# One accumulator on VectorE for the weighted sum of gathered expert rows, in place of two on three engines

## The chip, the cores and the metric

The kernel runs on one core of one Trainium2 chip. The metric is the device time of one execution in microseconds, the median of several runs.

## The reference

A backbone of two layers over 512 latent tokens with 256 context tokens, d = 1024. Each layer mixes tokens and then runs a product-key expert network (PEER) on each token: a router picks 16 of 16384 experts for each of 8 heads, 128 rows a token, and the token's output is a gated, weighted sum over them. That last step is what the change touches:

```python
u_e = u_tab[ib]                                   # ib: [tokens, 8, 16] of 16384 experts
v_e = v_tab[ib]
a = jax.nn.gelu(jnp.einsum('nd,nhkd->nhk', xb, u_e)) * gb
return jnp.einsum('nhk,nhkd->nd', a, v_e)
```

Layer 0 does it for latent and context tokens, layer 1 for latent tokens alone.

## The kernel before

**Two ways through the experts.** Most latent tokens take all 16384 experts, with a gate that is zero for the experts not picked: in layer 0 all 512 tokens (four tiles of 128), in layer 1 the first 384 (three tiles). The other tiles gather the rows that the router picked: the two context tiles in layer 0, the last latent tile in layer 1.

**The dense way** has two stages. `build_g` writes the gates of all experts to DRAM, with comparisons on VectorE (L1364, L1365), products on VectorE (L1366) and GpSimd or VectorE (L1370, `go`), and TensorE products in float16. `dense` then goes over 128 blocks of 128 experts. For each it loads `du` and `dv` (512 KB each), makes the two float32r parts of each (`duh` on ScalarE L1388, `dul` on VectorE L1389, `dvh` L1461, `dvl` L1462), and forms the activations `h` by 24 matmuls (`hidden`, L1394). Every fifth block's activations were made earlier, beside the routing, and are kept in DRAM; these 26 blocks load them as `dge` instead, so 102 blocks have the 24 matmuls. VectorE multiplies with the gates (`dcf`, L1469), ScalarE and VectorE make the two parts `dch` (L1472) and `dcl` (L1473), and TensorE multiplies with `v` into `o` (L142): 18 matmuls for three tiles of tokens into six PSUM banks, which stay there to the end. In layer 0 the fourth tile has no banks for that: `fourth()` (L1427) takes it for a pair of blocks at a time, in one bank, and VectorE adds the bank to `do` in SBUF (L1436) before the next use of the bank. That makes 24 matmuls of `o` a block in layer 0.

**The gathered way** runs in the background of both stages. `gather` (L1209) is a generator; a step of it issues the two indirect fetches of group n on GpSimd (L1258; a row of 8 KB for each of 128 tokens, u and v side by side in one `uv` tile), the products of group n-1 with the token (VectorE, L1240: an elementwise product over the u half with its sum into `dots`), gelu and gate (ScalarE L1244, VectorE L1252), and the weighted sum of group n-2. There are 128 rows a tile in groups of two, so 64 steps. Of each group, the even row is scaled by ScalarE in place (L1226) and added by GpSimd to `acc[1]` (L1227; the first row of the tile is written there by ScalarE alone, L1229); the odd row is scaled and added by VectorE in one instruction to `acc[0]` (L1232, first row L1234). After the last step VectorE joins the two (L1263), multiplies with the gate row (L1265) and adds the residual (L1267). The six `uv` buffers hold three groups.

**What sets the order.** Steps are called while the program of the stage is written: in `build_g` by a rate a piece of the gates (L1369), in `dense` after each block's `dch` and `dcl` so that all are done six blocks before the end (L1474 to L1477). A scheduler then sets the order of each engine's queue, and each engine runs its queue in order. `du` and `dv` and the other plain loads are issued by SyncE, the fetches by GpSimd.

Of the kernel before, what the change touches and what calls it, by code (L numbers as in the profile page):

```python
# [15 lines left out]
AF = mybir.ActivationFunctionType  # L16
OP = mybir.AluOpType
# [4 lines left out]
P = 128  # L22
D = 1024
# [18 lines left out]
# latent tokens whose experts are computed densely, per layer; the rest gathers expert rows  # L42
# [22 lines left out]
# candidate pairs (a, b) of two sorted lists with (a + 1)(b + 1) <= 16: (first a, number of a, number of b, offset)  # L65
# [10 lines left out]
def merge(*gens):  # L76
    """Steps of several generators in turn."""
    gens = list(gens)
    while gens:
        for g in list(gens):  # L80
            try:
                yield next(g)
            except StopIteration:
                gens.remove(g)


class Kern:
    def __init__(self, ctx, tc, a, dbg=None):
# [12 lines left out]
        self.split = lambda k: k % 2 == 0  # L101
# [43 lines left out]
    def tick(self, us):  # L145
        """Advance the background work by what fits beside `us` of foreground work."""
# [23 lines left out]
    def steps(self, n):  # L170
        """Advance the background work by n steps."""
        self.pace += n
        while self.pace >= 1.0:
            self.pace -= 1.0
            self.step()

    def flush(self):
        """Finish the gathers under way without starting others."""
# [5 lines left out]
    def advance(self, n):  # L184
        """Advance the second background work by n steps."""
# [29 lines left out]
    # ------------------------------------------------------------------ setup  # L215
# [34 lines left out]
    def xsrc(self, l, w, seg, i, cols=slice(0, D)):  # L250
        """Residual stream before sub-layer w of layer l: 128 tokens of a segment."""
# [15 lines left out]
    # -------------------------------------------------------------------- ada  # L267
    def ada(self, l, parts, pw, ps):
        """Modulation vectors: shifts and scales as columns, gates as rows in DRAM."""
# [10 lines left out]
        for part in parts:  # L280
            for half in range(2):
# [4 lines left out]
                # a quarter of the array for each of four blocks of the contraction  # L286
# [28 lines left out]
    # ------------------------------------------------------------ adaLN norms  # L315
    def parts(self, pool, src, cols, tag, eng, bufs):
        """Half a block of weights in the two parts that float32r products carry: a pair for each 128 rows."""
# [7 lines left out]
    def norm(self, l, w, seg, xT, xt=None, side=None, deep=2):  # L325
        """Modulated norm, channel-major, of the residual stream, in one part or two.

        xt: the stream [P, n / P, D] and partial sums of its squares [P, n / P, 4], where those are on chip."""
# [40 lines left out]
    # ------------------------------------------------------------- token mix  # L369
# [3 lines left out]
    def store(self, l, seg, full, st, m, alias=False):  # L373
        """What outlives the projections, in a pool for each of three stacks."""
# [25 lines left out]
    def projections(self, l, seg, full, m):  # L400
        """The projections of a segment, a generator that takes a block of weights in each step."""
# [17 lines left out]
    def latent(self, l, m):  # L419
        """The first layer's latent projections, then their attention where the projections' operand was."""  # L420
# [6 lines left out]
    def mlstm(self, l, seg, full, m):  # L427
        """The recurrence after the projections, a generator."""
# [12 lines left out]
    def project_ctx(self, l, m):  # L441
        """The context's new residual stream, to DRAM."""
# [20 lines left out]
    def project(self, l, m, px, sd, rest=()):  # L463
        """The latent tokens' new residual stream, to DRAM and to a pool, after the rest of their mixing."""
# [41 lines left out]
    def weights(self, l, full, pool):  # L506
        """Blocks of columns of w_in (256, the gates 100), each a step; half a block ahead of its use."""
# [20 lines left out]
    def mm3(self, out, lhs, rhs):  # L528
        """Contraction over blocks of operands that are given in two parts each."""
# [6 lines left out]
    def chan(self, w, c, m, x):  # L536
        """Channel-major projections of m columns from column c of the weight block."""
# [5 lines left out]
    def rows(self, w, i, x):  # L543
        """Token-major projections of a tile of tokens."""
# [5 lines left out]
    def tseq(self, ap, seg):  # L550
        """A channel-major row of a segment in its token order, viewed in time order."""
# [5 lines left out]
    # ----------------------------------------------------------------- mLSTM  # L557
    def ml_proj(self, l, seg, full, x, m):
        """Queries, keys, values and output gates, a generator."""
# [69 lines left out]
    def ml_gin(self, l, seg, x, m):  # L629
        """Gate preactivations in time order (reversed for the backward direction)."""  # L630
# [86 lines left out]
    def ml_core(self, l, seg, full, m):  # L717
        """Chunked recurrence of both directions, a generator."""
# [3 lines left out]
    def ml_chunks(self, st, l, seg, full, m):  # L722
# [14 lines left out]
        # recurrent states before each chunk, in the order of processing  # L737
# [124 lines left out]
    # --------------------------------------------------------------- pooling  # L862
# [42 lines left out]
    # ------------------------------------------------ neighbourhood attention  # L905
    def na_proj(self, l, seg, full, x, d):
        """Normalised queries (token-major) and keys (channel-major) and values, a generator."""
# [4 lines left out]
        with ExitStack() as st:  # L912
# [25 lines left out]
            # the keys' transposes come where the tensor engine need not wait for them  # L938
# [14 lines left out]
    def na_core(self, l, seg, d, sd):  # L953
        """Attention of all heads, a generator; each step's softmax runs beside the products of its neighbours."""
# [95 lines left out]
    # ------------------------------------------------------------------ PEER  # L1050
    def route(self, l, seg, xT, pr):
        """Product-key top-k of each token: expert ids [P, HK] and gates [P, HK] per tile."""
# [80 lines left out]
    def route_pick(self, pw, nt, sf, iv, iota, h0, ts, ef):  # L1133
        """Best TOPK pairs of RH heads from their sorted lists: scores and expert ids, in three steps."""
# [74 lines left out]
    def gather(self, pg, l, seg, i, xn, idx, gate):  # L1209
        """Experts of one tile of tokens by gathered rows, a generator over groups of experts."""  # L1210
# [458 lines left out]
```

## Time and profile before

| | |
|---|---|
| runs | 4574.12, 4580.28, 4576.12 us, median 4576.12 us |
| the profiled execution: its span | 4588.3 us (no other time of it is recorded) |
| TensorE matmul (PE) | 4041.2 us busy, 88% of the span |
| VectorE (DVE) | 3483.2 us, 76% |
| GpSimd (POOL) | 2233.7 us, 49% |
| ScalarE (ACT) | 1761.3 us, 38% |
| gathered fetches, their DMA queue | 406.35 MB, 24.2% of the 16 engines' span |

The profiled execution is 0.27% longer than the median of the runs. Busy times are sums over one execution; engines run beside each other. A matmul's record is longer than the distance to the next one, since matmuls overlap. PEclk is the clock that TensorE was granted, as a share of 2.4 GHz. The stages of interest are, in layer 0, the building of the gates up to 1302 us and the dense stage from 1302 to 2690; in layer 1 the same up to 3580 and from there to the end. A line of `L142` is that of a helper that issues most matmuls; the tile names tell them apart.

### The profile page before, as it was taken

The numbers are of one execution on the slowest core, as the hardware profiler recorded it, in microseconds if no ns is written. First come the engines' busy times: TensorE is split into PE (matmuls) and PEld (weight loads), VectorE is DVE, ScalarE is ACT, GpSimd is POOL, SyncE is SP. The second block draws the span as 40 slices with busy tenths as digits, with TensorE's granted clock in tenths as the row PEclk, the third lists the DMA queues.
The fourth block names the chain that finished last, engine by engine and source line by source line (L and its number), as shares of the span: only waits on it lengthen the run. The fifth ranks groups of instructions, "written<-read, shape, count | busy, mean of one in ns | idle before, by whom it ended". The sixth has DMA issues, their size and how long they took to land. (4 is left out here: it accounts for less than half of the span.)

```text
span 4588.3 us, 57862 instructions
## 1 busy us (share of the span) xinstructions
PE 4041.2 (88%) x20829; PEld 3367.6 (73%) x20829; DVE 3483.2 (76%) x6158; ACT 1761.3 (38%) x2754; POOL 2233.7 (49%) x1552
## 2 busy tenths in 40 slices
PE   6889777877779999999999979888868899999998
PEld 4568667756657777777777768677657788888887
DVE  2545675789979999889999855674889678887776
ACT  2332243335543333333333333343246344444343
POOL 2133355776645555455555333345866344444441
PEclk8889888988889999999999989988978999999999
DMA  7663212327778888788888633223256777777784
GB/s 270 215 211 93 81 48 82 94 94 227 219 268 303 323 316 317 301 316 316 322 316 317 257 113 109 63 73 98 71 171 206 263 294 291 286 301 296 277 304 166
DMA packets 429352, 996.51 MB, mean 217 GB/s; under 512 B 31448, under 2 KB 264280, under 8 KB 375816
## 3 DMA queue, kind: packets, MB, share of 16 engines
q1 hardware_dynamic: 372760, 586.46, 37.0%
q0 software_dynamic: 56304, 406.35, 24.2%
q8 instruction: 164, 2.69, 0.2%
q14 instruction: 124, 1.02, 0.1%
HBM read 909.97 MB, written 81.17 MB: 216 GB/s over the span
## 5 line engine op out<-in xcount | busy, mean ns | idle before, releaser
L1227 POOL TENSOR_TENSOR eacc<-eacc,uv 128x1024 f32<-128x1024 f32 x189 | 587.2, 3107 | 1074.1 <-ACT uv L1226 1013.4
L1240 DVE SCALAR_TENSOR_TENSOR uv<-uv,xn 128x1024 f32<-128x1024 f32 x384 | 849.8, 2247 | 0.0
L142 PE MATMUL o<-dvh,dch 128*128 128x512 f32 x1792 | 709.0, 396 | 72.3 <-DVE do L1436 53.2
L142 PE MATMUL o<-dvh,dcl 128*128 128x512 f32 x1792 | 706.0, 394 | 0.7 <-DVE dcl L1473 0.7
L142 PE MATMUL o<-dvl,dch 128*128 128x512 f32 x1792 | 704.9, 393 | 0.0
L1258 POOL DMA_INDIRECT uv<-in_peer_uv_dram,ridx x384 | 579.7, 1510 | 137.2 <-issue 75.0
L1394 PE MATMUL h<-xh,duh 128*128 128x512 f32 (+1 forms) x1632 | 607.7, 372 | 37.2 <-ACT duh L1388 35.8
L1394 PE MATMUL h<-xh,dul 128*128 128x512 f32 (+1 forms) x1632 | 607.6, 372 | 0.4 <-DVE dul L1389 0.3
L1394 PE MATMUL h<-xl,duh 128*128 128x512 f32 (+1 forms) x1632 | 606.0, 371 | 0.0
L142 PEld LDWEIGHTS o<-dvh,dch 128*128 128x128 f32 x1792 | 337.2, 188 | 162.1 <-DVE do L1436 64.6
L142 PEld LDWEIGHTS o<-dvh,dcl 128*128 128x128 f32 x1792 | 338.2, 189 | 86.9 <-DVE dcl L1473 14.6
L142 PEld LDWEIGHTS o<-dvl,dch 128*128 128x128 f32 x1792 | 337.5, 188 | 66.7 <-DVE dvl L1462 0.3
L1394 PEld LDWEIGHTS h<-xh,duh 128*128 128x128 f32 x1632 | 312.6, 192 | 80.4 <-ACT duh L1388 36.4
L1462 DVE TENSOR_TENSOR dvl<-dv,dvh 128x1024 fp32r<-128x1024 f32 x256 | 309.8, 1216 | 62.5 <-ACT dvh L1461 62.4
L1389 DVE TENSOR_TENSOR dul<-du,duh 128x1024 fp32r<-128x1024 f32 x204 | 249.5, 1224 | 135.0 <-ACT duh L1388 128.2
L1388 ACT CAST duh<-du 128x1024 fp32r<-128x1024 f32 x256 | 267.6, 1046 | 202.7 <-PE h L1394 102.1
L1394 PEld LDWEIGHTS h<-xl,duh 128*128 128x128 f32 x1632 | 312.1, 191 | 43.6
L1394 PEld LDWEIGHTS h<-xh,dul 128*128 128x128 f32 x1632 | 311.2, 191 | 39.7 <-DVE dul L1389 1.6
L142 PE MATMUL mm<-go,gob 128*128 128x128 f16 x1792 | 239.9, 297 | 96.9 <-DVE go L1366 85.4
L1244 ACT ACTIVATE egf<-dots 128x2 f32<-128x2 f32 x192 | 39.1, 204 | 734.8 <-DVE uv L1240 734.8
L1472 ACT CAST dch<-dcf 128x512 fp32r<-128x512 f32 (+1 forms) x256 | 145.2, 567 | 437.1 <-DVE dcf L1469 434.8
L1461 ACT CAST dvh<-dv 128x1024 fp32r<-128x1024 f32 x256 | 263.2, 1048 | 112.1 <-DMA dv<-in_peer_v_dram 63.4
(356 smaller groups left out, 8785.2 us busy)
## 6 DMA issues: line engine op xcount, KB each, us to landing
du<-in_peer_ut_dram SPq DMA_DIRECT2D x256, 512.0 KB
dv<-in_peer_v_dram SPq DMA_DIRECT2D x256, 512.0 KB
Gd<-gst SPq DMA_DIRECT2D x28, 2048.0 KB
wa<-in_w_ada_dram SPq DMA_DIRECT2D x24, 2048.0 KB
w<-in_w_in_dram SPq DMA_DIRECT2D x78, 512.0 KB
dG<-Gd SPq DMA_DIRECT2D x32, 1024.0 KB
w<-in_peer_wq_dram SPq DMA_DIRECT2D x48, 512.0 KB
dG<-Gd SPq DMA_DIRECT2D x32, 768.0 KB
```

Of the source, the lines that this page charges most:

```text
L142: self.nc.tensor.matmul(out, lhsT=lhsT, rhs=rhs, start=start, stop=stop)
L1227: nc.gpsimd.tensor_add(acc[1], acc[1], V)
L1240: nc.vector.scalar_tensor_tensor(t[:, :D], t[:, :D], 1.0, xn, op0=OP.mult, op1=OP.mult, accum_out=dots[:, k:k + 1])
L1244: nc.scalar.activation(ge, x, AF.Gelu_apprx_tanh)
L1258: nc.gpsimd.indirect_dma_start(t, None, a["peer_uv"], bass.IndirectOffsetOnAxis(ap=idx[:, k:k + 1], axis=0))
L1388: nc.scalar.copy(uh, u)
L1389: eng.tensor_sub(ul, u, uh.bitcast(F32))
L1394: nc.tensor.matmul(hp[:, :nd], lhsT=lt[:, k], rhs=rt[:, k, :nd], start=n == 0, stop=n == 3 * KD - 1)
L1461: nc.scalar.copy(vh, v)
L1462: nc.vector.tensor_sub(vl, v, vh.bitcast(F32))
L1472: m1 = nc.scalar.copy(ch, cf)
```

## The change

All rows of a gathered tile go to one accumulator. Each row is scaled and added by one VectorE instruction; ScalarE's scaling, GpSimd's addition, the second accumulator, the choice between them (`self.split`) and the joining addition are gone:

```diff
-        self.split = lambda k: k % 2 == 0
...
-        acc = [T(pg, [P, D], tag="eacc0"), T(pg, [P, D], tag="eacc1")]
-        used = [False, False]
+        acc = T(pg, [P, D], tag="eacc")
+        used = False
...
             for k, t, w in done:
-                V = t[:, D:]
-                if self.split(k):
-                    if used[1]:
-                        nc.scalar.activation(V, V, AF.Copy, scale=w)
-                        nc.gpsimd.tensor_add(acc[1], acc[1], V)
-                    else:
-                        nc.scalar.activation(acc[1], V, AF.Copy, scale=w)
-                    used[1] = True
-                elif used[0]:
-                    nc.vector.scalar_tensor_tensor(acc[0], V, w, acc[0], op0=OP.mult, op1=OP.add)
+                if used:
+                    nc.vector.scalar_tensor_tensor(acc, t[:, D:], w, acc, op0=OP.mult, op1=OP.add)
                 else:
-                    nc.vector.tensor_scalar_mul(acc[0], V, w)
-                    used[0] = True
+                    nc.vector.tensor_scalar_mul(acc, t[:, D:], w)
+                used = True
...
-        if used[1]:
-            nc.vector.tensor_add(acc[0], acc[0], acc[1])
         self.load(xn, self.grow[l][1][seg:seg + 1, :].to_broadcast([P, D]))
-        nc.vector.tensor_mul(acc[0], acc[0], xn)
+        nc.vector.tensor_mul(acc, acc, xn)
         self.load(xn, self.xsrc(l, 1, seg, i))
-        nc.vector.tensor_add(acc[0], acc[0], xn)
-        self.load(self.xdst(l, 1, seg, i), acc[0])
+        nc.vector.tensor_add(acc, acc, xn)
+        self.load(self.xdst(l, 1, seg, i), acc)
```

The rest of the diff empties comments. Lines behind the change stand some 11 lower: the product with the token is L1231 (before L1240), the multiply-add L1223 (L1232), the gate L1243 (L1252), the fetch L1249 (L1258), `do` L1425 (L1436), `dvl` L1451 (L1462), `dcl` L1462 (L1473).

Two places of the engines' queues show what moves. The first is VectorE in the dense stage of layer 0, one step of the gather; `eacc` is the accumulator, `uv` a gathered row, `egf` its weight. Before:

```order
L1473 TENSOR_TENSOR dcl_13903<-dcf_13900,dch_13902 128x512
L1232 SCALAR_TENSOR_TENSOR eacc_1861_8864<-uv_13750,egf_13836,eacc_1861_8864 128x1024
L1240 SCALAR_TENSOR_TENSOR uv_13839,dots_8863<-uv_13839,xn_4947 128x1024
L1240 SCALAR_TENSOR_TENSOR uv_13841,dots_8863<-uv_13841,xn_4947 128x1024
L1436 TENSOR_TENSOR do_2355_11271<-do_2355_11271,o_13944 128x512
L1462 TENSOR_TENSOR dvl_13955<-dv_13952,dvh_13954 128x1024
L1252 TENSOR_TENSOR egf_13911<-egf_13911,rgate_1077_4928 128x2
L1462 TENSOR_TENSOR dvl_14032<-dv_14029,dvh_14031 128x1024
```

With the change:

```order
L1462 TENSOR_TENSOR dcl_13861<-dcf_13858,dch_13860 128x512
L1223 SCALAR_TENSOR_TENSOR eacc_8864<-uv_13707,egf_13794,eacc_8864 128x1024
L1231 SCALAR_TENSOR_TENSOR uv_13797,dots_8863<-uv_13797,xn_4947 128x1024
L1223 SCALAR_TENSOR_TENSOR eacc_8864<-uv_13709,egf_13794,eacc_8864 128x1024
L1231 SCALAR_TENSOR_TENSOR uv_13799,dots_8863<-uv_13799,xn_4947 128x1024
L1425 TENSOR_TENSOR do_2354_11263<-do_2354_11263,o_13901 128x512
L1243 TENSOR_TENSOR egf_13868<-egf_13868,rgate_1077_4928 128x2
L1451 TENSOR_TENSOR dvl_13912<-dv_13909,dvh_13911 128x1024
L1451 TENSOR_TENSOR dvl_13988<-dv_13985,dvh_13987 128x1024
```

Each of the two products with the token now stands behind a multiply-add into the same accumulator, and the second multiply-add has one product between itself and the first.

The second is GpSimd in the dense stage of layer 0; in brackets are the semaphores of the engines and DMA queues that an instruction waits for. Before:

```order
L1227 TENSOR_TENSOR eacc_3169_15584<-eacc_3169_15584,uv_16759 128x1024 [waits DMASW0_49,Activation_49]
L1258 DMA uv_17002<-in_peer_uv_dram,ridx_1079_4936 128x2048 [waits DMASW1_49,DVE_49]
L1258 DMA uv_17004<-in_peer_uv_dram,ridx_1079_4936 128x2048 [waits Pool_49]
L1227 TENSOR_TENSOR eacc_3169_15584<-eacc_3169_15584,uv_16836 128x1024 [waits DMASW2_49,Activation_49]
L1258 DMA uv_17093<-in_peer_uv_dram,ridx_1079_4936 128x2048 [waits DMASW3_49,DVE_49]
```

With the change:

```order
L1249 DMA uv_16081<-in_peer_uv_dram,ridx_1079_4936 128x2048 [waits DMASW2_49,DVE_49]
L1249 DMA uv_16083<-in_peer_uv_dram,ridx_1079_4936 128x2048 [waits DMASW3_49,DVE_49]
L1249 DMA uv_16157<-in_peer_uv_dram,ridx_1079_4936 128x2048 [waits DMASW4_49,DVE_49]
L1249 DMA uv_16159<-in_peer_uv_dram,ridx_1079_4936 128x2048 [waits DMASW5_49,DVE_49]
L1249 DMA uv_16247<-in_peer_uv_dram,ridx_1079_4936 128x2048 [waits DMASW6_49,DVE_49]
```

Before, each pair of fetches stood behind an addition that waits for ScalarE; now fetches stand behind fetches, and each of them waits for VectorE itself.

## Rows read from the trace of the kernel before

**Rows 1.** Stretches: us; PE, PEld, DVE, ACT, POOL busy; PEclk, DMA, GB/s
```profile
1010.00:1302.00 292.00, 229.66 (x1395) 183.14 (x1395) 281.31 (x296) 164.78 (x192) 184.31 (x86) 0.87 0.72 221
1302.00:2690.00 1388.00, 1307.99 (x5520) 1052.05 (x5520) 1212.68 (x1347) 511.96 (x700) 702.63 (x365) 0.97 0.79 300
...
3580.00:4588.00 1008.00, 975.25 (x4752) 862.05 (x4752) 768.40 (x868) 408.79 (x583) 406.69 (x183) 0.99 0.75 277
```

**Rows 2.** Waits of PE, 1302 to 2690: us, times, longest
```profile
PE o L142 <- DVE do L1436: 53.2, 27, 3.1
PE h L1394 <- ACT duh L1388: 21.3, 1, 21.3
```

**Rows 3.** Groups of DVE, 1302 to 2690: busy us, mean ns, idle
```profile
L1240 DVE SCALAR_TENSOR_TENSOR uv<-uv,xn 128x1024 f32<-128x1024 f32 x238 | 537.5, 2293 | 0.0
...
L1232 DVE SCALAR_TENSOR_TENSOR eacc<-uv,egf,eacc 128x1024 f32<-128x1024 f32 x119 | 152.1, 1278 | 0.0
```

**Rows 4.** Timeline of DVE, one step: start us, us, line, tiles
```profile
1705.47 1.28 DVE L1232 SCALAR_TENSOR_TENSOR eacc<-uv,egf,eacc 128x1024 f32<-128x1024 f32 x1
1706.67 3.44 DVE L1240 SCALAR_TENSOR_TENSOR uv<-uv,xn 128x1024 f32<-128x1024 f32 x1
...
1710.04 1.21 DVE L1240 SCALAR_TENSOR_TENSOR uv<-uv,xn 128x1024 f32<-128x1024 f32 x1
1711.18 0.08 DVE L1240 DVE_READ_ACCUMULATOR uv<-uv,xn 128x1 f32 x1
```

**Rows 5.** Timeline of POOL beside it
```profile
1705.96 3.06 POOL L1227 TENSOR_TENSOR eacc<-eacc,uv 128x1024 f32<-128x1024 f32 x1 [5.82 <-ACT uv L1226]
```

**Rows 6.** Timeline of PE, two waits (idle before in brackets)
```profile
1713.22 0.50 PE L142 MATMUL o<-dvh,dch 128*128 128x512 f32 x1 [2.25 <-DVE do L1436]
...
1777.04 0.61 PE L142 MATMUL o<-dvh,dch 128*128 128x512 f32 x1 [2.61 <-DVE do L1436]
```

**Rows 7.** Timeline of DVE, the end of a gathered tile
```profile
1925.76 1.22 DVE L1263 TENSOR_TENSOR eacc<-eacc,eacc 128x1024 f32<-128x1024 f32 x1
1927.01 1.23 DVE L1265 TENSOR_TENSOR eacc<-eacc,xn 128x1024 f32<-128x1024 f32 x1
```

**Rows 8.** Timeline of PE, the ends of one block's `h` products
```profile
1683.19 0.40 PE L1394 MATMUL h<-xh,duh 128*128 128x512 f32 x1
...
1688.80 0.40 PE L142 MATMUL o<-dvh,dch 128*128 128x512 f32 x1
```

**Rows 9.** Chain of waits: 36 products of `o`; start us, us
```profile
3625.38 8.20 PE o L142 x36
```

**Rows 10.** Stretches in layer 0, columns as in rows 1
```profile
1777.30:1780.70 3.40, 3.40 (x9) 2.61 (x9) 3.40 (x3) 2.67 (x3) 2.53 (x1) 0.50 0.94 343
1780.70:1883.10 102.40, 98.22 (x425) 79.33 (x425) 94.29 (x107) 38.03 (x55) 56.87 (x30) 1.00 0.84 321
2000.00:2020.00 20.00, 18.25 (x80) 14.54 (x79) 16.87 (x17) 7.04 (x9) 9.19 (x6) 1.00 1.01 404
```

**Rows 11.** Groups of POOL, 3580 to 4588
```profile
L1227 POOL TENSOR_TENSOR eacc<-eacc,uv 128x1024 f32<-128x1024 f32 x62 | 186.6, 3009 | 533.2 <-ACT uv L1226 520.0 <-issue 13.2
```

**Rows 12.** Waits of PE, 3580 to 4588
```profile
PE o L142 <- ACT dch L1472: 15.7, 24, 1.2
```

**Rows 13.** Chain of waits, 3998 to 4080
```profile
4008.20 4.49 DVE uv L1240 x4
...
4014.24 8.39 DMA dge<-H
...
4034.09 4.52 PE o L142 x18
```

**Rows 14.** Groups of POOL, 1010 to 1302
```profile
L1227 POOL TENSOR_TENSOR eacc<-eacc,uv 128x1024 f32<-128x1024 f32 x7 | 19.9, 2838 | 1.3 <-DVE go L1366 1.3
```

**Rows 15.** Timeline of DVE in layer 1
```profile
4012.61 1.21 DVE L1462 TENSOR_TENSOR dvl<-dv,dvh 128x1024 fp32r<-128x1024 f32 x1
```

**Rows 16.** Timeline of POOL in layer 1
```profile
4012.67 1.97 POOL L1258 DMA_INDIRECT uv<-in_peer_uv_dram,ridx  x1 [0.30 <-issue]
```

## The prediction

> **What bounds the kernel now.** I read the stretches first [rows 1]: the gathers run in two pairs of stages, the building of the dense gates and then the dense experts, once a layer. In the dense stage of layer 0 (1302 to 2690 us) VectorE is busy 1212.7 of 1388 us and the clock share is 0.97; in that of layer 1 (from 3580) it is busy 768.4 of 1008 and the clock is 0.99. TensorE is the longest engine in both, so the next view is what it waits for. In layer 0 that is 53.2 us in 27 waits for `do`, VectorE's addition of the fourth token tile, beside one wait of 21.3 us at the start [rows 2]. So VectorE, in its order, sets the end there.
>
> What VectorE does in that time is in the groups by form [rows 3]: 238 products with the token (L1240) at a mean of 2293 ns, against 119 multiply-adds into the accumulator (L1232) of the same size at 1278 ns. The timeline of one step shows why [rows 4]: of two equal products the first takes 3.44 us, the second 1.21. GpSimd's addition starts at 1705.96 and takes 3.06, to 1709.02 [rows 5]; the first product starts inside it and ends at 1710.11, 1.1 us after it, which is about its own length. VectorE stands while GpSimd adds. The step of VectorE from L1232 to the end of the second product is 1.20 + 3.37 + 1.14 = 5.71 us from start to start (1705.47, 1706.67, 1710.04, 1711.18 in [rows 4]). TensorE waits for the queue behind it: it has stood 2.25 us for `do` at 1713.22, and 64 us later it has stood 2.61 us once more [rows 6].
>
> **The change part by part.** *Removed:* three tiles of 64 steps each lose a scaling on ScalarE and an addition on GpSimd a step (189 additions, since a tile's first row only starts the sum), and a joining addition each. ScalarE is not what is waited for, so its part is worth nothing by itself. GpSimd's part is worth the stall: 3.37 - 1.14 = 2.23 us in each step. *Added: one multiply-add on VectorE in each step*, 1.20 us from start to start [rows 4]. The new order of a step is accumulator, product, accumulator, product: 1.20 + 1.14 + 1.20 + 1.14 = 4.68 us, or 1.03 us less than 5.71.
>
> The second multiply-add reads what the first wrote, and now waits for it; a product of 1.14 us lies between them. The nearest row is a dependent pair with nothing between: 1.22 us long, the next starts 1.25 us after [rows 7], so the wait costs 0.1 us at most, and I take 0. Behind it stand only the step's own second product and `do`.
>
> *Moved: the gathers.* Each step's two fetches stood behind GpSimd's addition; now GpSimd holds nothing else in the dense stages and each fetch waits for the buffer that VectorE's multiply-add gives back, one step earlier. So they are issued earlier. In the building stages a fetch that waits does hold the `go` products behind it on GpSimd, as the additions did.
>
> *The dense stage of layer 0.* Full pace: 24 products of `h` take 5.61 us (1683.19 to 1688.80) [rows 8], 36 of `o` 8.20 us [rows 9]. The code issues 102 x 24 and 128 x 24 of them (5520, as [rows 1] has it): 102 x 5.61 + 3072 x 8.20 / 36 = 572 + 700 = 1272 us. The stage has 1388 - 21.3 = 1367, so 95 us are lost. A period of ten blocks of experts, from the end of one stretch at half clock to the end of the next (1674.9 to 1780.7, 105.8 us [rows 10]), has ten steps and about 6.5 us of loss: the two waits, 4.9, and 1.6 behind the second, where the clock is at half (1.2 GHz) for 3.4 us [rows 10]. VectorE gains 10.3 us in it; 6 of the steps lie between the two waits and 4 ahead of the first, so 6.2 stand against the 2.61 and 4.1 against the 2.25. Both go, and TensorE becomes the bound with some 4 us of slack in ten blocks. Thirteen periods would be 85; the start and the change of the gather's tile, near the 1925 of [rows 7], keep theirs, and I take **-78** (bounds: -95 if nothing is lost, -40 if half of each wait comes back).
>
> *The dense stage of layer 1.* There are 62 additions [rows 11] in 128 blocks, VectorE has room, and TensorE waits 15.7 us in 24 times, 1.2 at most [rows 12]. The chain of waits shows from where: two products (4.49), the load of a kept activation (8.39), a second pair of products like the first, then TensorE, whose next 18 products take 4.52 us, 0.4 more than half of the 36 [rows 9, 13]. Some 0.3 for each of the 24 makes 23 us in all. Both steps on that chain get 1.03 shorter, and the waits have a mean of 0.65. I take **-20** (bounds -23 and -5).
>
> *The building stages.* VectorE is busy 281 of 292 us in that of layer 0, with 7 of the additions, 2.84 us each [rows 1, 14]. Each stalls it by up to 2.2 and each new multiply-add costs 1.2, which the other additions of GpSimd there can stall too. Between -10 and +10, for both layers I take **-4**.
>
> Sum: -78 - 20 - 4 = **-102 us** on a span of 4588.3, which is 12.2 us (0.27%) over the median of the runs. From the median: 4576.1 - 102 = **4474 us**.
>
> A rule against the change has to be weighed. What the rows show is VectorE above 85% busy in layer 0, and stalled by the engine that takes work off it. The Trainium skill, Perfetto Trace Analysis, section Optimizing Scalar/DVE Operations, says that work of a saturated VectorE may well go to ScalarE or GpSimd, though between VectorE and GpSimd it might not help, since they share a read port. By its first half the change should cost 181 x 1.2 = 217 us of VectorE's time (the slower rival below), by its second half little or nothing (the rival of no change); the rows of this case go further than either, to a gain.
>
> **The rivals.** *Slower: the stall stays.* If something else on GpSimd holds VectorE as the additions did, the step gets 1.20 us longer. That something could only be the fetches, which GpSimd still issues. All of it would lie on the path in layer 0 (119 x 1.2 = 143), two steps of each of 13 periods in layer 1 (31) and some 15 in the building: 4576 + 189 = 4765 us. It decides as soon as less than 1.20 of the 2.23 us go. Against it: VectorE's subtraction at 4012.61 takes 1.21 us [rows 15] beside a fetch that GpSimd issues from 4012.67 for 1.97 [rows 16], no longer than the second product of [rows 4] does with the same number of elements. I give it 6%.
>
> *Half of the gain: the transfers come late.* A period moves 321 GB/s at a DMA share of 0.84 [rows 10]; at the new pace that is 321 x 105.8 / 99.3 = 342 and 0.89, and fetches are issued at other moments. For it: the chain of layer 1 has a load of 8.39 us between its two steps [rows 13]. Against it: 20 us at 404 GB/s have been moved [rows 10]. If the loads of kept activations (26 in layer 0, every fifth block) come 2 us later, 52 us return: 4474 + 52 = 4526 us. 17%.
>
> *No change:* the waits move from `do` to another product of VectorE, say the ScalarE-VectorE pair that makes `dch` and `dcl`. Each period must then lose its 6.5 us anew, 4576 us; nothing in the rows has that size. 4%. *More:* all of the 95 and 23, with 10 in the building, 4448 us or a little below: 5%.
>
> **How the numbers follow.** The forecast, 4450 to 4500 us, has 68%. The range, 4440 to 4535, leaves out the slower rival, the one of no change, and a part of the late transfers. A measurement of this kernel can tell 0.2%, 9 us, from no change. Faster 0.90, same 0.04, slower 0.06.
>
> **What would show it.** L1231, the product with the token in the changed kernel, at a mean near 1.22 us and none of 3.4 in the dense stages; the multiply-add twice as often at 1.28; TensorE's waits for `do` from 53.2 to under 10 us and the clock of that stage at 0.99 or more; its waits for `dch` in layer 1 from 15.7 to under 5; the stages 80 and 20 us shorter. Wrong would be: products still at 3.4 us beside fetches only (the slower rival); products short, but TensorE waiting as long for something else, named by its waits, or VectorE waiting for `dge` loads more than now (late transfers); a gain in the dense stages that the building takes back.

## The result, and the profile after

The changed kernel takes 4478.6 us (median of 4 runs, 4476.2 to 4482.9), the kernel before on the same chip 4577.0: the ratio is 0.9784, 95% interval 0.9771 to 0.9798, or 98 us less. The sum on record was 102 less, 4474.

The span of the profiled execution is 4474.4 us against 4588.3. These are the stretches of the changed kernel, from the first gate comparison of a layer to its first product `h`, and from there to the last `o` (in layer 1 to the end of the execution; columns as in [rows 1]):

```profile
1012.40:1317.50 305.10, 223.53 (x1387) 179.86 (x1386) 271.92 (x284) 154.61 (x179) 169.13 (x77) 0.84 0.72 229
1317.50:2612.00 1294.50, 1283.36 (x5520) 1039.83 (x5520) 1087.10 (x1460) 385.69 (x577) 394.16 (x245) 0.99 0.84 317
...
3286.70:3500.00 213.30, 157.41 (x1060) 139.16 (x1060) 187.73 (x184) 115.09 (x135) 120.37 (x53) 0.83 0.69 217
3500.00:4474.40 974.40, 962.28 (x4752) 867.36 (x4752) 703.17 (x929) 351.03 (x519) 199.55 (x121) 0.99 0.77 285
```

and the same four of the kernel before:

```profile
1015.80:1321.70 305.90, 226.32 (x1386) 180.44 (x1384) 278.23 (x275) 163.24 (x186) 182.14 (x84) 0.85 0.74 229
1321.70:2688.00 1366.30, 1307.96 (x5520) 1052.05 (x5520) 1209.38 (x1342) 509.80 (x697) 702.09 (x364) 0.98 0.79 300
...
3370.00:3584.60 214.60, 157.10 (x1060) 138.47 (x1060) 186.83 (x182) 116.56 (x136) 122.27 (x54) 0.83 0.70 216
3584.60:4588.30 1003.70, 975.24 (x4752) 862.03 (x4752) 767.29 (x868) 406.70 (x581) 406.69 (x183) 0.99 0.75 277
```

| stretch, us | before | after | difference | forecast |
|---|---|---|---|---|
| building, layer 0 | 305.9 | 305.1 | -0.8 | -4 for both |
| dense, layer 0 | 1366.3 | 1294.5 | -71.8 | -78 |
| building, layer 1 | 214.6 | 213.3 | -1.3 | |
| dense, layer 1 | 1003.7 | 974.4 | -29.3 | -20 |
| the rest | 1697.8 | 1687.1 | -10.7 | 0 |

The rest holds none of the gather's work on VectorE, and the change leaves its code alone. Its two parts take 1015.8 and 682.0 us before, 1012.4 and 674.7 after. In the traces of the eleven experiments that leave its code alone too, they came out between 1006 and 1014 us and between 671 and 684, so most of the 10.7 can be scatter between two executions; the 1015.8 lies 2 us above what the others have. With the rest counted in, the spans differ by 113.9 us; the medians differ by 98.4.

VectorE's groups in the dense stage of layer 0 answer to [rows 3]:

```profile
L1223 DVE SCALAR_TENSOR_TENSOR eacc<-uv,egf,eacc 128x1024 f32<-128x1024 f32 x239 | 305.9, 1280 | 0.0
L1231 DVE SCALAR_TENSOR_TENSOR uv<-uv,xn 128x1024 f32<-128x1024 f32 x238 | 289.9, 1219 | 0.0
```

The product with the token, L1231, has a mean of 1219 ns where it had 2293; twice as many multiply-adds stand beside it at 1280. One step of it, against [rows 4]:

```profile
1592.34 1.27 DVE L1223 SCALAR_TENSOR_TENSOR eacc<-uv,egf,eacc 128x1024 f32<-128x1024 f32 x1
1593.54 1.22 DVE L1231 SCALAR_TENSOR_TENSOR uv<-uv,xn 128x1024 f32<-128x1024 f32 x1
...
1594.68 1.28 DVE L1223 SCALAR_TENSOR_TENSOR eacc<-uv,egf,eacc 128x1024 f32<-128x1024 f32 x1
1595.88 1.22 DVE L1231 SCALAR_TENSOR_TENSOR uv<-uv,xn 128x1024 f32<-128x1024 f32 x1
1597.02 0.08 DVE L1231 DVE_READ_ACCUMULATOR uv<-uv,xn 128x1 f32 x1
```

From 1592.34 to 1597.02 are 4.68 us, as worked out. VectorE's busy time in the stage fell from 1209.4 to 1087.1 us, by 122.3; 119 steps of 1.03 us are 122.6. TensorE's waits there, against [rows 2]:

```profile
PE h L1383 <- ACT duh L1377: 23.5, 1, 23.5
PE h L1383 <- ACT dge L1386: 7.6, 3, 3.5
PE o L141 <- DVE do L1425: 3.5, 2, 3.4
```

The 53.2 us for `do` are 3.5. In layer 1, against [rows 12], the 15.7 us for `dch` are gone from the list; what stays is the start of the stage:

```profile
PE h L1383 <- ACT duh L1377: 16.4, 1, 16.4
```

### The profile page after: what moved, and what is told of

It is laid out like the page before. It is cut to its first block, busy times and chain, and to the rows that moved or that the text cites. A ratio compares the mean times of both kernels' runs of the same rounds, so it can differ in the third digit from the quotient of the medians.

```text
span 4474.4 us, 57073 instructions
## 1 busy us (share of the span) xinstructions
PE 3992.0 (89%) x20829; PEld 3352.4 (75%) x20829; DVE 3283.9 (73%) x6347; ACT 1571.2 (35%) x2562; POOL 1705.1 (38%) x1363
## 5 line engine op out<-in xcount | busy, mean ns | idle before, releaser
L1249 POOL DMA_INDIRECT uv<-in_peer_uv_dram,ridx x384 | 633.3, 1649 | 1558.2 <-DVE eacc L1223 1506.8
L1223 DVE SCALAR_TENSOR_TENSOR eacc<-uv,egf,eacc 128x1024 f32<-128x1024 f32 x381 | 492.4, 1293 | 0.0
L1231 DVE SCALAR_TENSOR_TENSOR uv<-uv,xn 128x1024 f32<-128x1024 f32 x384 | 470.3, 1225 | 0.0
L1451 DVE TENSOR_TENSOR dvl<-dv,dvh 128x1024 fp32r<-128x1024 f32 x256 | 308.8, 1221 | 101.5 <-ACT dvh L1450 82.1
L141 PEld LDWEIGHTS <-gob 128*128 128x128 f16 x1792 | 194.8, 120 | 141.4 <-DVE go L1355 100.6
L1365 ACT ACTIVATE gst<-mm 128x512 f32<-128x512 f32 x224 | 226.3, 1120 | 166.3 <-PE mm L141 153.6
```

Of the source, the lines that this page charges most:

```text
L141: self.nc.tensor.matmul(out, lhsT=lhsT, rhs=rhs, start=start, stop=stop)
L1223: nc.vector.scalar_tensor_tensor(acc, t[:, D:], w, acc, op0=OP.mult, op1=OP.add)
L1231: nc.vector.scalar_tensor_tensor(t[:, :D], t[:, :D], 1.0, xn, op0=OP.mult, op1=OP.mult, accum_out=dots[:, k:k + 1])
L1249: nc.gpsimd.indirect_dma_start(t, None, a["peer_uv"], bass.IndirectOffsetOnAxis(ap=idx[:, k:k + 1], axis=0))
L1365: nc.scalar.activation(stage[:, :, q * 8 + g * 4:q * 8 + g * 4 + 4].rearrange("p i t -> p t i"), gp.rearrange("p (t i) -> p t i", i=P), AF ...
L1451: nc.vector.tensor_sub(vl, v, vh.bitcast(F32))
```

## The experiments

Two theories stood against each other. **Theory 1**: VectorE stands while GpSimd's addition reads SBUF, and the gain is that stall less the added multiply-add. **Theory 2**: the gain comes from the queues, since the fetches stood behind a chain from ScalarE to GpSimd, or from ScalarE's relief. All ratios are to the kernel before in runs of the same chip.

### A GpSimd addition put back, at no fixed place

```diff
+        z = T(pg, [P, D], tag="ez")
+        nc.gpsimd.memset(z, 0.0)
...
+            if done:
+                nc.gpsimd.tensor_add(z, z, z)
```

> The changed kernel with one GpSimd addition of a scratch tile to itself (128x1024, some 3 us, two operands read from SBUF) put back into each step; it depends on nothing of the gather. Theory 1 (VectorE stands while GpSimd adds, and the gain was that stall): a step costs VectorE 4.7 + 2.2 = 6.9 us instead of 4.7, so layer 0's dense stage has some 119 x 2.2 = 260 us more of VectorE and becomes its again: slower than the kernel before, 4600 to 4740 us, with products or multiply-adds of 3.4 us. Theory 2 (the gain was that the fetches no longer stand behind a chain from ScalarE to GpSimd): the addition waits for nothing, so 4478 to 4500 us.

Measured: 4739.6 us, ratio 1.0358 (1.0341 to 1.0376). It is inside what theory 1 said and far from theory 2, but the additions did not run where I meant them to. They depend on nothing, and the scheduler put all but 9 of the 192 into the building stages and the first 200 us behind each (GpSimd's instructions on the scratch tile in the two building stages; the columns are us, busy us and count, clock, DMA share, GB/s):

```profile
1006.80:1396.20 389.40, 148.34 (x66) 0.71 0.57 179
...
3466.30:3757.10 290.80, 125.72 (x57) 0.70 0.51 159
```

So they slowed what stood there: the building stages took 389 and 291 us instead of 305 and 213. That a free GpSimd addition costs VectorE time is shown, its price in the dense stage is not. The next but two puts it in its old place.

### GpSimd kept as busy, without reading

```diff
...
+            if done:
+                for _ in range(3):
+                    nc.gpsimd.memset(z, 0.0)
```

> The changed kernel with three GpSimd memsets of a scratch tile in each step (128x1024 each, together some 2.85 us of GpSimd, nothing read from SBUF). Theory 1 (it is GpSimd's reading beside VectorE that stalls): no long products, 4478 to 4490 us. Rival (any GpSimd work of that length in the queue of the fetches does it): as slow as the kernel with the scratch addition, 4600 or more.

Measured: 4471.5 us (4463.7 to 4480.4), ratio 0.9777 (0.9760 to 0.9793), as the change. The memsets did run in the dense stage, 311 of them in layer 0:

```profile
1300.90:2595.40 1294.50, 297.49 (x311) 0.99 0.84 317
```

Only 6 of them stood beside a product or a multiply-add. But 222 stood beside `dul` or `dvl`, VectorE's subtractions, which read two tensors of the same size, and none of these took longer than 1.23 us. One place, GpSimd and then VectorE:

```profile
1712.52 3.00 POOL L1231 MEMSET ez<- 128x1024 f32 x3
```

```profile
1714.04 1.22 DVE L1456 TENSOR_TENSOR dvl<-dv,dvh 128x1024 fp32r<-128x1024 f32 x1
```

In the kernel with the scratch additions the same subtractions were long where those had gathered (1396 to 1600 us):

```profile
L1455 DVE TENSOR_TENSOR dvl<-dv,dvh 128x1024 fp32r<-128x1024 f32 x13 | 26.8, 2084 | 11.5 <-ACT dvh L1454 11.5
```

The stage is 1294.5 us long with the memsets and without. Occupying GpSimd in the queue of the fetches costs nothing; theory 2's queue is out. What stalls is tied to what the addition does and a memset does not. That this is its reading is the likely part, but no run here parts the reading from the rest of an addition's work. The Trainium skill, SBUF — State Buffer, section Who interferes with whom, says that a VectorE instruction with two inputs in SBUF contends with a GpSimd instruction that reads SBUF and not with one that only writes it. The traces of these two kernels agree: 1.22 us for `dvl` beside memsets, a mean of 2.08 among additions.

### ScalarE's scaling kept

```diff
-                if used:
+                if used and k % 2 == 0:
+                    nc.scalar.activation(t[:, D:], t[:, D:], AF.Copy, scale=w)
+                    nc.vector.tensor_add(acc, acc, t[:, D:])
+                elif used:
                     nc.vector.scalar_tensor_tensor(acc, t[:, D:], w, acc, op0=OP.mult, op1=OP.add)
```

> The changed kernel with the even rows scaled by ScalarE in place again and then added by VectorE (a plain addition in place of the multiply-add). Theory 1: ScalarE's part was worth nothing, 4478 us within 10. Theory 2 (the chain over ScalarE was the cost): a third or more of the 98 us comes back, 4510 us or more.

Measured: 4466.4 us (4464.2 to 4475.0), ratio 0.9763 (0.9746 to 0.9779): 12 us less than the change, where 10 either way were allowed, and nothing of theory 2's loss. ScalarE's part was worth nothing. The 12 us lie in the dense stage of layer 0:

```profile
1315.00:2597.50 1282.50, 1278.36 (x5520) 1038.27 (x5520) 1077.98 (x1460) 507.39 (x696) 328.70 (x245) 1.00 0.86 320
```

1282.5 us against 1294.5. They come from what happens around the switch from one gathered tile to the next. In the changed kernel TensorE stands there three times and runs some products at half clock behind each (0.63 us instead of 0.39); two of the three, with the idle time before in brackets:

```profile
1883.96 0.50 PE L141 MATMUL o<-dvh,dch 128*128 128x512 f32 x1 [3.38 <-DVE do L1425]
...
1885.49 0.63 PE L1383 MATMUL h<-xh,duh 128*128 128x512 f32 x1
```

```profile
2017.28 0.50 PE L1383 MATMUL h<-xh,duh 128*128 128x512 f32 x1 [3.45 <-ACT dge L1386]
```

Behind each of the three is a load that came late. Ahead of the first, VectorE stood for a kept activation; ahead of the other two, ScalarE stood for the weights `du`, and its `dge`, which TensorE waits for, comes next in its queue:

```profile
1879.68 0.69 DVE L1458 TENSOR_TENSOR dcf<-dge,dG 128x512 f32<-128x512 f32 x1 [3.34 <-DMA dge<-H]
```

```profile
1971.68 1.04 ACT L1377 CAST duh<-du 128x1024 fp32r<-128x1024 f32 x1 [8.86 <-DMA du<-in_peer_ut_dram]
2015.68 1.04 ACT L1377 CAST duh<-du 128x1024 fp32r<-128x1024 f32 x1 [9.61 <-DMA du<-in_peer_ut_dram]
```

With ScalarE's scaling kept, no wait of ScalarE for `du` in this stage is longer than 0.2 us; in the kernel before none is longer than 1.14. So the change brought these two late loads with it, and by the starts of TensorE's products the two places cost 10 us. SyncE issued them 8 and 9 us ahead of the `duh` that reads them, where the median of the stage is 20; by the trace it was VectorE, in its order, that released them. Why that order lets the loads go late in one kernel and not in the other was not tried.

### The stall put back, at its old place

Against the kernel of the last experiment:

```diff
...
                     nc.vector.tensor_add(acc, acc, t[:, D:])
+                    nc.gpsimd.tensor_add(z, z, t[:, D:])
```

> The kernel with ScalarE's scaling and VectorE's addition of the even rows, and beside it GpSimd adds the same scaled row to a scratch tile that nobody reads, at the place in its queue where its addition stood before. Only that addition differs from the kernel without it (4466 us). Theory 1 (VectorE stands while GpSimd adds, up to 2.2 us each): VectorE's step is 4.7 + 2.2 = 6.9 us, layer 0's dense stage gets 119 x 2.2 = 260 us more of VectorE and 130 to 260 us longer, layer 1's 30 to 60: 4620 to 4760 us, slower than the kernel before, with VectorE's 128x1024 instructions near 3.4 us beside the additions. Theory 2 (the gain came from another place: ScalarE, the queue of the fetches): within 20 us of 4466.

Measured: 4672.1 us, ratio 1.0205 (1.0187 to 1.0224); 206 us more than without that line, though nobody reads what it adds up. The dense stage of layer 0:

```profile
1333.00:2757.60 1424.60, 1330.77 (x5520) 1062.89 (x5520) 1333.87 (x1460) 508.73 (x696) 662.00 (x365) 0.96 0.79 288
```

VectorE is busy 1333.9 us in layer 0 instead of 1078.0: 255.9 for 119 additions, 2.15 each. TensorE then waits again, and the clock share of the stage falls to 0.96. The stall now falls on VectorE's addition of the scaled row, which waits for ScalarE as GpSimd's does and so runs beside it (a mean of 1219 ns without GpSimd's), and no longer on the products:

```profile
L1226 DVE TENSOR_TENSOR eacc<-eacc,uv 128x1024 f32<-128x1024 f32 x119 | 404.4, 3399 | 0.0
L1237 DVE SCALAR_TENSOR_TENSOR uv<-uv,xn 128x1024 f32<-128x1024 f32 x238 | 288.8, 1214 | 0.0
```

One such place, VectorE and then GpSimd:

```profile
1711.08 3.41 DVE L1226 TENSOR_TENSOR eacc<-eacc,uv 128x1024 f32<-128x1024 f32 x1
```

```profile
1710.43 2.97 POOL L1227 TENSOR_TENSOR ez<-ez,uv 128x1024 f32<-128x1024 f32 x1 [5.26 <-ACT uv L1225]
```

GpSimd's addition ends at 1713.40, VectorE's at 1714.49, 1.09 us after it. In 118 of the 119 places VectorE's instruction ends 1.08 or 1.09 us after GpSimd's. This settles it for theory 1.

### The even rows left out

```diff
                 if self.split(k):
+                    continue
```

> The kernel before with the even rows left out of the weighted sum (no scaling, no GpSimd addition, and no multiply-add on VectorE in their place; half of the sum is missing). Theory 1: the dense stages are TensorE's once the stall is gone, so the 181 added multiply-adds there are covered; only those of the building stages, some 8 to 15 us, are saved: 4455 to 4475 us. Rival (the added multiply-adds lie on the path, and the gain is the stall less their cost): 98 plus a good part of 189 x 1.2 = 227 us below the kernel before, under 4430 us.

Measured: 4445.8 us (4438.0 to 4455.6), ratio 0.9712 (0.9692 to 0.9733). Lower than I expected, above the rival. The added multiply-adds cost at most 33 us of the 227 that they take on VectorE: 14 in the building of layer 0 and 17 in its dense stage; layer 1's stages are as with the change.

```profile
1304.90:2582.10 1277.20, 1275.76 (x5520) 1038.10 (x5520) 948.04 (x1340) 383.15 (x577) 315.66 (x244) 1.00 0.85 320
1013.40:1304.90 291.50, 220.43 (x1384) 178.36 (x1382) 261.41 (x276) 156.15 (x182) 170.74 (x79) 0.85 0.76 244
```

So "covered" was right for all but a seventh, and the seventh sits in the building stage and at the switch of the tile. Even that is not sure to be their price. The 17 us are about what the three places at the switch cost the changed kernel, and neither of its two late loads of `du` occurs here. And the building stage of the kernel with the memsets, which has every multiply-add, came out at 294.8 us, so that most of the 14 can be scatter.

### Half of the additions

```diff
-        self.split = lambda k: k % 2 == 0
+        self.split = lambda k: k % 4 == 0
```

> The kernel before with every fourth row instead of every second on ScalarE and GpSimd, so half of the additions. Theory 1: each of them that goes frees 1.03 us of VectorE in its step and takes its stall away. Half of the gain or a bit more, since VectorE's shortage in layer 0 was 6.5 of 105.8 us a period and 5 of the 10.3 come back: 4500 to 4535 us. Rival (GpSimd's chain over ScalarE, which stays in the queue of the fetches in every second step): above 4550.

Measured: 4494.7 us, ratio 0.9815 (0.9798 to 0.9833). It is 5 us below the range: half of the additions gone give 81 of the 98 us. The dense stage of layer 0, and the mean of the products, which is halfway:

```profile
1316.30:2619.20 1302.90, 1282.46 (x5520) 1038.43 (x5520) 1148.21 (x1402) 447.83 (x637) 550.26 (x304) 1.00 0.83 315
```

```profile
L1240 DVE SCALAR_TENSOR_TENSOR uv<-uv,xn 128x1024 f32<-128x1024 f32 x238 | 415.7, 1765 | 0.0
```

I read this as a shortage: once VectorE's queue is just short enough, more relief buys little.

### The change in layer 1 alone

```diff
-                if self.split(k):
+                if l == 0 and self.split(k):
```

> The change made in layer 1 alone; layer 0 keeps the split. Theory 1 with the loss read from the stages (layer 1's dense stage lost 34 us before and 5 after): 4577 - 30 = 4547 us, between 4538 and 4555. Rival (what layer 1 gained comes from layer 0, through transfers or the clock): within 10 of 4577. Third: the sum on record had 20 + 2 here, 4555.

Measured: 4544.4 us (4541.3 to 4551.6), ratio 0.9933 (0.9914 to 0.9951), 31 us. The two dense stages are those of the kernel before and of the changed one, to some us:

```profile
1312.00:2675.40 1363.40, 1303.06 (x5520) 1048.41 (x5520) 1208.86 (x1342) 510.06 (x697) 703.35 (x364) 0.98 0.80 301
3567.80:4541.40 973.60, 961.55 (x4752) 866.66 (x4752) 702.81 (x929) 350.99 (x519) 199.25 (x121) 0.99 0.77 286
```

### Two accumulators, both on VectorE

```diff
-                        nc.scalar.activation(V, V, AF.Copy, scale=w)
-                        nc.gpsimd.tensor_add(acc[1], acc[1], V)
+                        nc.vector.scalar_tensor_tensor(acc[1], V, w, acc[1], op0=OP.mult, op1=OP.add)
...
-                        nc.scalar.activation(acc[1], V, AF.Copy, scale=w)
+                        nc.vector.tensor_scalar_mul(acc[1], V, w)
```

> All rows on VectorE as in the change, but in two accumulators, even and odd rows apart, joined at the end as before: no multiply-add reads what the one ahead of it wrote. Theory 1 (a product lies between the two dependent multiply-adds, so the dependence costs nothing): 4478 us within 10; three joins more are 4 us, covered. Rival (VectorE waits for its own result): 119 to 181 times 0.1 to 0.3 us less, and the rest of layer 0's loss with it, 4450 to 4468.

Measured: 4471.6 us (4471.0 to 4477.2), ratio 0.9767 (0.9751 to 0.9783). Within the 10 us, above the rival's range; the dense stage of layer 0 takes 1290.8 us, with the schedule a little different again. The dependence of the multiply-adds costs nothing that can be told.

### The same cure in the building stages

The building stages had gained nothing, and VectorE's rows there, in the changed kernel's layer 0, show why they could:

```profile
L1355 DVE TENSOR_TENSOR go<-goa,e 128x1024 f16<-128x1024 f16 x64 | 98.2, 1534 | 0.0
...
L1359 DVE TENSOR_TENSOR go<-goa,e 128x1024 f16<-128x1024 f16 x21 | 14.3, 680 | 0.0
```

Both are 128x1024 in float16, as the comparison L1353 is. Beside GpSimd's own L1359 (two of three) and `dul`, L1355 and L1353 have means of 1.53 and 0.98 us; the L1359 that VectorE does itself, every third, has 0.68. TensorE's waits up to the end of that stage say which of the two engines holds it:

```profile
PE mm L141 <- DVE go L1355: 48.4, 32, 5.7
...
PE mm L141 <- POOL go L1359: 5.5, 6, 1.5
```

```diff
-                (nc.vector if n % 3 == 0 else nc.gpsimd).tensor_tensor(o2, oa, bc(e16[3]), op=OP.mult)
+                nc.vector.tensor_tensor(o2, oa, bc(e16[3]), op=OP.mult)
...
-            ge = self.hidden(l, c, pool, pool, xh, xl, "sm", self.nc.gpsimd)
+            ge = self.hidden(l, c, pool, pool, xh, xl, "sm", self.nc.vector)
```

> The changed kernel with the same cure in the building stages: the second gate product (go, two of three on GpSimd) and the low parts of the early blocks' weights (dul) all on VectorE. Theory 1: VectorE's three products of each piece have means of 0.98, 0.88 and 1.53 us in the changed kernel against 0.68 undisturbed, some 90 us of stall in layer 0's stage and some 70 in layer 1's; the moved work adds 43 x 0.6 + 14 x 1.15 = 42 and 32 x 0.6 + 12 x 1.15 = 33. 40 to 90 us faster than the changed kernel: 4390 to 4440 us. Rival (VectorE, 95% busy there, is the bound, and 127 more instructions on it cost their own length): 75 us or more slower, 4550 us.

Measured: 4445.1 us (4430.4 to 4447.4), ratio 0.9701 (0.9679 to 0.9724), 5 us above the range and far from the rival. All gate products take 0.68 us now, and the two building stages 281.6 and 196.1 us. But layer 0's stage starts 14 us later (1026.4), and the kept blocks' `sm` products, which were done before the gates' last, end 34 us after them. Then only the first change of that diff, with `dul` left to GpSimd:

> The changed kernel with only the second gate product (go) moved to VectorE; the low parts of the early blocks' weights (dul) stay on GpSimd. Theory 1: the 75 stalls by go end (most of the 90 and 70 us), at 75 x 0.6 = 45 us of moved work; the 26 additions of dul in the two stages go on stalling by some 2 us each. The stages get 25 to 40 us shorter each in VectorE; TensorE, 216 of 238 us busy in that of the kernel with both moved, keeps it from more: 4415 to 4450 us. Rival (it was dul alone that stalled): within 10 of 4478.

Measured: 4396.9 us (4388.9 to 4397.5), ratio 0.9607 (0.9581 to 0.9633); 18 us better than the best that I expected. The two building stages, 305.1 and 213.3 in the changed kernel:

```profile
1007.40:1263.10 255.70, 211.86 (x1385) 168.97 (x1383) 227.33 (x326) 157.61 (x182) 74.86 (x35) 0.87 0.85 274
3237.60:3422.50 184.90, 149.16 (x1060) 130.54 (x1060) 153.55 (x217) 117.09 (x135) 41.80 (x21) 0.85 0.80 250
```

```profile
L1359 DVE TENSOR_TENSOR go<-goa,e 128x1024 f16<-128x1024 f16 x64 | 48.5, 758 | 0.0
```

VectorE has 64 instructions L1359 where it had 21 and is busy 227.3 us where it was 271.9; TensorE waits 25 us for its gate products instead of 48. The rival, that `dul` alone had stalled, is out by 82 us. Two of GpSimd's 14 `dul` last over 6 us now, the others 2.4 to 2.9, and no wait of TensorE in the stage is for them; the kept blocks are done by 1182, well before the gates. Why their place differs so between these two kernels was not tried.

With ScalarE's scaling and the gate product as above, and of `dul` only that of the building stages on VectorE:

```diff
...
+                self.late = True
                 self.build_g(s1, l, r)
             run(self.bg2 or ())
+            self.late = False
...
-            ge = self.hidden(l, c, pool, pool, xh, xl, "sm", self.nc.gpsimd)
+            ge = self.hidden(l, c, pool, pool, xh, xl, "sm", self.nc.vector if self.late else self.nc.gpsimd)
```

> The version that the runs point to: even rows scaled by ScalarE and added by VectorE (4466 us alone), the second gate product on VectorE, and dul on VectorE in the building stages but on GpSimd beside the routing, where moving it had put the start of layer 0's building stage 14 us later. If the gains add: 4466 - 33 - 14 = 4419 us, 4400 to 4435. If TensorE bounds the building stages whatever VectorE does there, the 33 of the kernel with both moved is all: 4433 to 4450.

Measured: 4403.8 us (4401.2 to 4407.6), ratio 0.9626 (0.9601 to 0.9651). Inside the range of adding gains, but slower than the version that leaves `dul` on GpSimd. Last, that version with ScalarE's scaling (the diff of that experiment and the one of `go` together):

> The kernel with the second gate product on VectorE (4397 us), and with even rows scaled by ScalarE and added by VectorE, which was 12 us faster than the multiply-adds by the order around the switch of the gathered tile in layer 0. If that order comes out again: 4385 us, 4378 to 4392; if it was an accident of that schedule: 4397 within 6.

Measured: 4392.1 us (4384.7 to 4395.0), ratio 0.9588 (0.9572 to 0.9604), the lowest median. It lies on the upper end of the range for the order coming out again and inside the range for an accident. In the trace the order did come out again, with no late load of `du`: the stage has 1282.8 us where the version without the scaling has 1297.8. But of these 15 us only 5 are to be seen in the medians, and the runs of the two overlap: between the two versions nothing is decided.

```profile
1269.30:2552.10 1282.80, 1278.54 (x5520) 1038.25 (x5520) 1078.50 (x1460) 507.59 (x696) 328.81 (x245) 1.00 0.85 320
```

## Why the prediction was right

**The price of a step** held to the hundredth: 1.20 + 1.14 + 1.20 + 1.14 = 4.68 us, products at 1.22, no long ones. The stall of 2.23 us that it took from one step is 2.15 as a mean of 119 (the stall put back).

**Layer 0's dense stage**: -72 for -78. Both waits of each period went. Of the 95 us of loss some 22 stay (1294.5 against the pure pace of 1272); by the starts of TensorE's products 4 of them lie in the slow start and 15 at the three places around the switch of the tile. I had put 17 aside for these, but not for the reason that the runs showed: I had them as losses that the kernel before has already, and 10 of them are two late loads that came with the change.

**Layer 1's dense stage** is the mis-sized term: -29 for -20, outside its bounds. The term was the loss, taken as 15.7 us of waits and 0.3 us in the products behind each. By the pure pace (24 products of `h` with 384 columns take 4.24 us in the chain of waits, so 102 x 4.24 + 2304 x 8.20 / 36 = 957 us) TensorE lost 34 from 3584.6 to its last product at 4576.2, and 5 after the change. The starts of TensorE's products say where: the waits that the profile lists behind the start have 16 us, the products behind each of these 25 cost 0.42 us and not 0.3 (10 us), and 3.6 us lay in delays of some 0.12 us between products, which no list of waits shows and the sum didn't have. All three are gone after the change; the slow start stays (3 us before, 4 after). That all of the waits and of the loss behind them went was right. One of the 25 waits:

```profile
4015.27 0.39 PE L142 MATMUL o<-dvh,dcl 128*128 128x512 f32 x1
4016.20 0.50 PE L142 MATMUL o<-dvh,dch 128*128 128x512 f32 x1 [0.54 <-ACT dch L1472]
```

From start to start are 0.93 us where undisturbed products have 0.23: 0.54 of wait and 0.16 more, and the nine products behind it lose 0.26 besides. The pure pace of `h`:

```profile
4059.41 4.24 PE h L1394 x24
```

**The building stages**: -2 for -4. Stalls gone and multiply-adds added cancel there, as the sum had it. What the sum didn't see is that the same stall, by GpSimd's gate products, was worth some 80 us in these stages.

**The 10 us that lay over** by spans are in the rest, most likely scatter; the medians are 4 us from the sum. That it came so close is in part luck: layer 0 gave 6 us less than forecast and layer 1 gave 9 more.

**The rivals.** The slower one fell: 345 of the 477 products and multiply-adds in the dense stage of layer 0 run beside a fetch, and none of them is longer than 1.29 us. The late transfers fell at the price that I gave them: from 1400 to 1700 us the changed kernel moves 337 GB/s at a share of 0.89 (worked out were 342 and 0.89), and VectorE waits 3.3 us for `dge` loads in the stage where it waited 5.6. On a small scale they came all the same, by other loads than I named: the two of `du` at the switch, 10 us. The waits that were to move to another product (no change) didn't.

The rule that I weighed, in the Trainium skill, Perfetto Trace Analysis, section Optimizing Scalar/DVE Operations, allows work of a saturated VectorE to go to GpSimd and doubts that it helps. Here it does harm: an addition that saves VectorE 1.20 us stalls it by 2.15.

## What to carry to other kernels

Work that is given to GpSimd to relieve VectorE should be priced in VectorE's own rows: where one instruction of a form lasts 1.2 us and another 3.4, and the long ones overlap a GpSimd instruction that reads SBUF, the help costs more than it saves. Move the instruction to VectorE when its own length there is below the stall, first in the stage whose longest engine waits for VectorE; look for the same pattern in other stages, since here the second place was worth nearly as much as the first. And expect the gain to stop at the next bound: half of the additions gave four fifths of it.

## What the hardware showed

- A GpSimd memset of 128x1024 (0.96 us) doesn't stall VectorE's `dul` and `dvl` of the same size (at most 1.23 us beside 222 of them). An addition or subtraction of that size stalls VectorE's instruction with two inputs to its end. With nothing of VectorE beside it GpSimd's takes 1.89 us (the scratch tile with itself) or 2.35 to 2.40 (`dul`); the additions of the kernel before, beside VectorE, have 3.0.
- The stall hits small instructions as hard as large ones, and also some that read one tensor only. The gate product of 128x2 elements takes 0.15 us by itself:

```profile
1099.73 2.73 DVE L1243 TENSOR_TENSOR egf<-egf,rgate 128x2 f32<-128x2 f32 x1
```

GpSimd's `dul` ran from 1100.03 to 1102.43 beside it. The first row's multiply, which reads one tensor and a column of weights, takes 0.74 us in two of its three places, with no addition, subtraction or product of GpSimd beside it, and 2.89 in the third, where a `dul` ran from 3402.77 to 3405.63:

```profile
3403.28 2.89 DVE L1225 TENSOR_SCALAR eacc<-uv,egf 128x1024 f32<-128x1024 f32 x1
```

- It can go the other way (the first row here is the `dul` of the point above). While VectorE ran gate products with no gap, GpSimd's `dul` lasted 6.15 us, and VectorE's kept their 0.68 until its first idle gap, at 1110.3:

```profile
1100.03 2.40 POOL L1378 TENSOR_TENSOR dul<-du,duh 128x1024 fp32r<-128x1024 f32 x1
1106.40 6.15 POOL L1378 TENSOR_TENSOR dul<-du,duh 128x1024 fp32r<-128x1024 f32 x1 [3.97 <-ACT duh L1377]
```

```profile
1109.61 0.68 DVE L1353 TENSOR_TENSOR goa<-e,iota 128x1024 f16<-128x1024 f16 x1
1110.75 2.35 DVE L1354 TENSOR_TENSOR gob<-e,iota 128x1024 f16<-128x1024 f16 x1 [0.46 <-PE mm L141]
```

What decides which engine waits was not tried.
